# A two-layer encoder on one core: recurrent pairs back to back, neighbourhood values by four units, start stage in runs

## Chip, cores, metric

One NeuronCore of a Trainium2 chip runs the whole program in one launch. The metric is device time in microseconds (us), the median of several executions.

## What is computed

The input x is 1024 tokens by 1024 features, float32. Two residual layers follow each other, and a final RMS norm:

```python
h = rms_norm(x) * (1 + scale(c)) + shift(c)
x = x + gate(c) * mixer(h)          # shift, scale, gate: 1024x1024 products with silu(c)
# layer 0: differential attention (4 heads) beside a bidirectional RG-LRU (512 channels)
xc = conv4(xb);  a = exp(-8 * sigmoid(Wa xc) * softplus(-lam));  u = sqrt(1 - a*a) * sigmoid(Wx xc) * xc
y  = scan_forward(a0, u0) + scan_backward(a1, u1)
# layer 1: 16 heads of 2-D neighbourhood attention, 8 x 16 window, per-head bias
p  = softmax(q k^T * scale + bias + mask);  o = p v
# each group times silu of its own projection, then an output projection
```

The result has to keep float32 accuracy, so every product is made of three matmuls on operands split in a high and a low part (`mm3`, L196-199).

## The kernel before

Activations lie transposed, features on partitions, so a projection of 128 output features over 512 tokens is 8 steps of three matmuls 128x512 into one PSUM bank (24 matmuls, called a slab half here; a slab has two halves). Weights come as slabs 128x1024 (`raw`): ScalarE (ACT) rounds the high part (`whi`, L181), GpSimd (POOL) subtracts for the low part (`wlo`, L182). VectorE (DVE) and ACT take the results out of the banks. The order of each engine follows the order in which the code issues instructions, changed by `tc.high_priority` and `tc.issue_after`; a `Feed` of generators gives projections out in pieces between other work (`pump(ns)` gives pieces worth so many ns), and `weave` alternates the pieces of several generators.

The stages, with the times of the profiled execution:

- **Start, 0 to 79 us.** x is loaded; `squares` (L470) makes the sums of squares of each half of the tokens with squares on ACT or DVE in `SQ` = 4 buffers and matmuls against a column of ones into 32 rows each (`ss_add`, L321); `spread` (L350) copies the reciprocal roots to all partitions through the constant `sel`. `mod_first(g)` (L255), for g = 0 to 3, loads eight pieces of the modulation weights (`ada`) and multiplies each with c into 32 rows, piece by piece. `parts` makes the normalized, modulated and split activations (`ahi`, `alo`), `products` (L499) the products of the first three slabs: xb0, xb1 (recurrent input) and v0.
- **Recurrent branch, 79 to 242 us.** For each of four chunks of 128 channels: `conv` (L630) on DVE; `pair` (L661) takes two chunks: gate products into banks, sigmoid and tanh on ACT into tiles `t`, `w` of one ring of `LR` = 12 buffers (a pair holds 12), then exp, square, sqrt on ACT and multiplies and scans (L707 to L714) on DVE. `gb(c)` is the projection for the silu gate of a chunk, which multiplies the scanned result (L605, L722) and stores it to DRAM. `xb(c)` is the projection that gives a chunk's input, `vj(h)` that of a head's values, `kq0` that of the first head's keys and queries, `mods` sums of later modulations on DVE. The order is the list `jobs`:

```python
jobs = [weave(pair((0, 1)), chain(xb(2), xb(3))), cv(2), cv(3), vj(1), vj(2),
        gb(0), gb(1), weave(pair((2, 3)), chain(vj(3), kq0()), mods(...)), gb(2), gb(3)]
```

- **Differential attention** to 500 us and the first output layer to 640 us.
- **Neighbourhood attention, 640 to 1128 us.** 64 units (8 pairs of heads, two halves of the tokens, four blocks). `na_a(u)` makes the logits of two heads and the softmax on DVE, ACT and POOL; `na_b(u)` transposes the six 128-column tiles (`etr`, L1202) and copies them to `et`, one head on DVE (L1208), the other on ACT (L1206); `na_c(u)` multiplies them with the values into 64 columns of the array for each head (`no`, L1226), six matmuls a unit. The loop over u issues na_a(u+1), a pump of 1700 ns, na_b(u), a pump, na_c(u-1), a pump.
- **Second output layer** to the end.

Matmuls of `norm`, `mod` and `no` (and a few others) use a part of the array's columns, 32 or 64; those of projections, gates, logits and transposes use all 128. A run below is a row of such narrow matmuls with no other between them.

Of the kernel before, what the change touches and what calls it, by code (L numbers as in the profile page):

```python
# [27 lines left out]
SQ = 4  # L28
# [68 lines left out]
def kernel(ctx, tc, xT, xTp, small, lamp, adaw, tb, w0, gw, wo0, w1, nab, wo1, out):  # L97
# [28 lines left out]
    sel = const.tile([P, 4, P], F32, tag="sel", name="sel")  # L126
    G.memset(sel[:], 1.0)
    G.affine_select(sel[:], sel[:], pattern=[[-32, 4], [0, P]], base=0, channel_multiplier=1,
                    compare_op=ALU.is_equal, fill=0.0)
# [3 lines left out]
                    compare_op=ALU.is_equal, fill=0.0)  # L133

# [120 lines left out]
    def mod_first(g, pool, small, c32):  # L255

        ps = ptp.tile([P, HF], F32, tag="pt", name=f"mod{g}")

        def sums(x, w, start, stop):
            for n in range(4):  # L260
                cols = x[:, n // 2, (n % 2) * P:(n % 2 + 1) * P]
                state["modmm"] = T.matmul(ps[32 * n:32 * n + 32, :P], w, cols,
                                          start=start, stop=stop)

        for k in range(KC):
# [3 lines left out]
            sums(piece, c32[:, k, :], k == 0, k == KC - 1)  # L269
        row = pool.tile([P, P], F32, tag="mrow", name="mrow", bufs=2)  # L270
        A.activation(row[:], ps[:, :P], AF.Copy)
        pc = ps[:, P:]
        T.matmul(pc[:, :4], row[:], pick[:], start=True, stop=True)
        m = small.tile([P, 2, 2], F32, tag=f"first{g}", name=f"first{g}", bufs=1)
        gain = small.tile([P, 2], F32, tag=f"gain{g}", name=f"gain{g}", bufs=1)
        b = sm[:, O_ADAB:O_ADAB + 2 * KC].rearrange("p (t k) -> p t k", t=2)
        V.tensor_tensor(m[:], pc[:, :4].rearrange("p (t j) -> p t j", t=2),
                        b[:, :, 2 * g:2 * g + 2], ALU.add)
        V.scalar_tensor_tensor(gain[:], m[:, 1, :], 1.0, sm[:, O_NG + 2 * g:O_NG + 2 * g + 2],
                               ALU.add, ALU.mult)  # L280
        for j in range(2):
            first_mod[2 * g + j] = gain[:, j:j + 1], m[:, 0, j:j + 1]
# [38 lines left out]
    def ss_add(ss, sq, start, stop, w=P):  # L321
        for j in range(4):
            T.matmul(ss[32 * j:32 * j + 32, :w], ones[:], sq[:, j * w:(j + 1) * w],
                     start=start, stop=stop)
# [25 lines left out]
    def spread(rr, bc, w=P):  # L350
        for j in range(4):
            T.matmul(bc[:, j * w:(j + 1) * w], sel[:, j, :], rr[:, :w], start=True, stop=True)
# [105 lines left out]
    with tc.tile_pool(name="start", bufs=2) as stp, tc.tile_pool(name="ada0", bufs=12) as adp:  # L458
        mixp[1] = stp
        for k in range(KC):  # L460
            mix_tile(k, f"xT{k}")
# [8 lines left out]
        def squares(hf, on_dve, pool, tag):  # L470
            for k in range(KC):
                state["x"] = nc.sync.dma_start(half(k, hf), xT[k * P:(k + 1) * P,
                                                               hf * HF:(hf + 1) * HF])
            ss = nbank[hf] = pool.tile([P, HF], F32, tag=tag, name=f"norm{hf}")
            for k in range(KC):
# [5 lines left out]
                ss_add(ss, sq, k == 0, k == KC - 1)  # L481
# [17 lines left out]
        def products(i, g, hf):  # L499
# [7 lines left out]
            for k in (2 * g, 2 * g + 1):  # L507
                mm3(banks[i, hf], ready[i][0][:, k, :], ready[i][1][:, k, :],
                    hact[k, hf][0][:], hact[k, hf][1][:], k == 0, k == KC - 1)
# [17 lines left out]
        products(2, 0, 0)  # L527
        with tc.issue_after(state["x"].ins):
            mod_first(2, adp, stp, c32)
        for i in range(3):  # L530
            products(i, 0, 1)
        for g in range(1, KC // 2):
# [5 lines left out]
            for n in range(6):  # L538
                i, hf = divmod(n, 2) if g == KC // 2 - 1 else (n % 3, n // 3)
                products(i, g, hf)  # L540
        for i, evac in enumerate((evac_xb(0), evac_xb(1), evac_v(0))):
            for hf in range(2):
                evac(hf, banks[i, hf])
        ahead(3)
# [81 lines left out]
    with tc.tile_pool(name="lru", bufs=1) as lp:  # L626
# [3 lines left out]
        def conv(c):  # L630
# [4 lines left out]
            eng = V if c < 2 else G  # L635
            eng.tensor_scalar(xc[:], x[:], cw(2), sm[:, O_CB + c:O_CB + c + 1], ALU.mult, ALU.add)
# [7 lines left out]
            V.tensor_copy(xh[:], xc[:])  # L644
# [89 lines left out]
        def weave(*jobs):  # L734

            jobs = list(jobs)
            while jobs:
                for job in tuple(jobs):
# [3 lines left out]
                    else:  # L742
# [17 lines left out]
    with ExitStack() as l0:  # L760
        ap = l0.enter_context(tc.tile_pool(name="attn", bufs=1))
        vtok = {}

# [267 lines left out]
    with tc.tile_pool(name="bound", bufs=2) as bp:  # L1031
        run, tail = out_layer(0, ato0, xTp, x1d, bp, [4, 5, 6, 7, 0, 1, 2, 3], by_tile,
# [33 lines left out]
    with ExitStack() as l1:  # L1066
# [46 lines left out]
        def load_ahead(p, w8):  # L1113

            if f"1v{p + 1 - (p + 1) % 2}" in feed.done:
                for b in range(min(4, w8 - 1)):
                    load_v(p + 1, b)
# [32 lines left out]
        def load_bias(u):  # L1150
            if u == 8 * NA_PAIRS:
                return
# [3 lines left out]
            bias["next"] = ap.tile([P, 2, 384], F32, tag="bias", name="bias")  # L1156
            nc.sync.dma_start(bias["next"][:, :, :n],
                              nab[2 * p:2 * p + 2, hf, :, BLK_B[b]:BLK_B[b] + n].rearrange(
                                  "h p n -> p h n"))

        def na_a(u):
# [14 lines left out]
            e = ap.tile([P, 2, 384], F32, tag="e", name="e")  # L1176
# [4 lines left out]
            for m in range(2):  # L1181
                state["dve"] = V.tensor_tensor_reduce(  # L1182
                    out=e[:, m, :n], in0=ps[:, m, :n], in1=bias["now"][:, m, :n], scale=-1.0,
# [10 lines left out]
        def na_b(u, e):  # L1194
# [4 lines left out]
            et = ap.tile([P, 2, 384], F32, tag="et", name="et", bufs=2)  # L1199
# [4 lines left out]
            for m in range(2):  # L1204
                if m:
                    A.activation(et[:kn, m, :], pt[:kn, m, :384], AF.Copy)  # L1206
                else:
                    V.tensor_copy(et[:kn, m, :], pt[:kn, m, :384])  # L1208
            return et

        def na_c(u, et):
            p, w8 = divmod(u, 8)
            hf, b = divmod(w8, 4)
            kn = 4 * BLK_W[b]
            if w8 == 0:
                feed.upto(f"1v{p - p % 2}")
                for n in range(4):
                    load_v(p, n)
                if p == 0:
                    feed.pump(5000.0)  # L1220
            if b == 0:
                ob[0] = ptp.tile([P, HF], F32, tag="pt", name=f"no{u}")
            po = ob[0]
            for j in range(3):
                for m in range(2):
                    T.matmul(po[64 * m:64 * m + 64, b * P:(b + 1) * P],  # L1226
                             vch[p, b][:kn, j + hf, 64 * m:64 * m + 64],
                             et[:kn, m, j * P:(j + 1) * P], start=(j == 0), stop=(j == 2))
            if b == 3:
                if late(p):  # L1230
                    if hf == 0:
                        mix_tile(p, f"o1_{p}")
                    A.activation(mixed[p][:, hf * HF:(hf + 1) * HF], po[:], AF.Copy)
                    written.add((p, hf))
                    gate1(p, hf)
                else:
                    feed.upto(f"1g{p}")
                    m = mixed[p][:, hf * HF:(hf + 1) * HF]
                    V.scalar_tensor_tensor(m, po[:], 0.5, m, ALU.mult, ALU.mult)
            load_ahead(p, w8)  # L1240
# [4 lines left out]
        for u in range(n_units + 1):  # L1245
            if u + 1 < n_units:
# [4 lines left out]
            feed.pump(PUMP1 if u < 56 else 800.0)  # L1251
            if u:
                na_c(u - 1, ets.pop(u - 1))
            feed.pump(PUMP1 if u < 56 else 800.0)
# [5 lines left out]
    with tc.tile_pool(name="fin", bufs=2) as fp:  # L1260
# [6 lines left out]

        segments = ((0, 0, 0, 512), (0, 1, 0, 256), (0, 1, 256, 512))
# [109 lines left out]
```

## Time and profile before

| | |
|---|---|
| median of 3 runs | 1229.72 us (1228.05 to 1231.03) |
| profiled execution | 1229.11 us, its span 1227.2 us |
| mean granted TensorE clock | 0.995 |
| PE (matmul) busy | 96% of the span, 7232 instructions |
| DVE, ACT, POOL busy | 59%, 45%, 31% |

The profiled execution is 0.05% under the median and has 1.9 us around its span. PE's ends are modelled and successive matmuls overlap in the record, so PE's pace is read from start to start, and a stall from the idle time that stands in square brackets ahead of an instruction, with the instruction that released it.

### The profile page before, as it was taken

The page shows a single profiled execution, that of the slowest core. Times are in us where ns is not written, and L with a number is a line of the kernel's source. Part 1 is how long each engine was busy: PE and PEld are TensorE (multiplying, and loading weights), DVE is VectorE, ACT ScalarE, POOL GpSimd, SP SyncE. Part 2 cuts the span into 40 slices and gives each one's busy share as a digit, 9 for nine tenths or more (in the row PEclk, how much of TensorE's full clock was granted, in tenths as well). Part 3 has the DMA queues.
Part 4 walks back from the last instruction along what each step waited for, and adds up shares of the span by engine and source line. Part 5 has one row for each costly group of instructions (what it writes and reads, how often), then busy time and mean ns, then how long its engine had stood idle before and what let it go on. Part 6 is the DMA issues. An engine that isn't in the chain of part 4 may idle for free.

```text
span 1227.2 us, 19073 instructions
## 1 busy us (share of the span) xinstructions
PE 1177.9 (96%) x7232; PEld 969.2 (79%) x7232; DVE 725.6 (59%) x1418; ACT 553.5 (45%) x1023; POOL 376.3 (31%) x348
## 2 busy tenths in 40 slices
PE   4989999799999999999999999999999999999997
PEld 3578887678888888777778888888988898877896
DVE  6762966899899889668672433453333323464344
ACT  3337658456666556423342333443344324375121
POOL 2113432133243334533422323333323333244100
PEclk9999999999999999999999999999999999999999
DMA  9610153232123110286424443333332333223312
GB/s 330 188 38 27 60 170 105 69 101 78 42 63 108 46 57 20 84 284 205 149 72 149 124 145 109 117 116 108 100 108 81 103 105 106 76 81 113 136 69 70
DMA packets 81467, 132.24 MB, mean 108 GB/s; under 512 B 7008, under 2 KB 48096, under 8 KB 81376
## 3 DMA queue, kind: packets, MB, share of 16 engines
q1 hardware_dynamic: 81376, 131.03, 34.1%
q8 instruction: 57, 0.93, 0.3%
q14 instruction: 34, 0.28, 0.1%
HBM read 110.03 MB, written 14.68 MB: 102 GB/s over the span
## 4 chain that ended last, share of the span: by engine, by line
PE 82%; DVE 10%; DMA 3%; ACT 2%; POOL 1%; issue 1%; SPq 0%; DVEq 0%; ACTq 0%; POOLq 0%
PE pp L197 16%; PE pp L199 16%; PE pp L198 15%; PE no L1226 4%; PE etr L1202 3%; PE v L197 3%; PE v L198 2%; PE v L199 2%; PE atr L857 2%; PE s L599 2%; PE s L600 2%; PE n L599 2%; PE n L600 2%; PE o L198 1%; PE o L197 1%
## 5 line engine op out<-in xcount | busy, mean ns | idle before, releaser
L197 PE MATMUL pp<-ahi,whi 128*128 128x512 f32 (+1 forms) x1040 | 405.9, 390 | 3.7 <-DVE sgb L605 3.3
L199 PE MATMUL pp<-ahi,wlo 128*128 128x512 f32 (+1 forms) x1040 | 397.4, 382 | 2.5 <-POOL wlo L182 2.5
L198 PE MATMUL pp<-alo,whi 128*128 128x512 f32 (+1 forms) x1040 | 395.8, 381 | 0.0
L182 POOL TENSOR_TENSOR wlo<-raw,whi 128x1024 fp32r<-128x1024 f32 x80 | 196.1, 2454 | 333.5 <-ACT whi L181 330.0
L197 PEld LDWEIGHTS pp<-ahi,whi 128*128 128x128 f32 x1040 | 196.3, 189 | 45.8 <-issue 9.6
L199 PEld LDWEIGHTS pp<-ahi,wlo 128*128 128x128 f32 x1040 | 196.3, 189 | 41.1 <-POOL wlo L182 3.4
L198 PEld LDWEIGHTS pp<-alo,whi 128*128 128x128 f32 x1040 | 196.5, 189 | 32.2 <-issue 0.7
L1182 DVE CUSTOM_DVE_ANT_0 e<-n,bias 128x288 f32<-128x288 f32 (+1 forms) x128 | 60.4, 504 | 151.8 <-PE n L600 76.7
L181 ACT ACTIVATE whi<-raw 128x1024 fp32r<-128x1024 f32 x80 | 84.3, 1055 | 133.4 <-PE pp L198 88.2
L1190 POOL TENSOR_SCALAR e<-e,r 128x288 f32<-128x288 f32 (+1 forms) x128 | 72.3, 577 | 180.0 <-DVE r L1188 178.0
L1185 ACT ACTIVATE e<-e,nm 128x288 f32<-128x288 f32 (+1 forms) x128 | 72.8, 570 | 111.9 <-DVE nm L1182 111.2
L831 ACT ACTIVATE e<-e,nm 128x1024 f32<-128x1024 f32 x64 | 73.4, 1148 | 38.3 <-DVE nm L827 37.7
L827 DVE CUSTOM_DVE_ANT_0 e<-s,tb 128x1024 f32<-128x1024 f32 x64 | 76.9, 1216 | 3.9 <-DMA tb<-in_tb_dram 2.6
L197 PE MATMUL v<-whi,ahi 128*128 128x256 f32 x256 | 74.7, 292 | 0.0
L198 PE MATMUL v<-wlo,ahi 128*128 128x256 f32 x256 | 72.5, 283 | 0.0
L199 PE MATMUL v<-whi,alo 128*128 128x256 f32 x256 | 72.3, 282 | 0.0
L848 POOL TENSOR_SCALAR e<-e,r 128x256 f32<-128x256 f32 x32 | 32.9, 1028 | 100.6 <-DVE r L837 42.4
L1226 PE MATMUL no<-et,vc 96*64 96x128 f32 (+1 forms) x768 | 60.6, 282 | 0.0
L1226 PEld LDWEIGHTS no<-et,vc 96*64 96x64 f32 (+1 forms) x768 | 42.2, 136 | 21.5 <-issue 19.3
L864 ACT ACTIVATE ath<-atr 128x512 fp32r<-128x512 f32 x64 | 38.0, 596 | 45.7 <-PE atr L857 45.4
L1206 ACT ACTIVATE et<-etr 96x384 f32<-96x384 f32 (+1 forms) x64 | 31.2, 487 | 58.8 <-DVE et L1208 53.7
L962 DVE SCALAR_TENSOR_TENSOR xh<-pp,mod,xh 128x512 f32<-128x512 f32 (+1 forms) x40 | 25.7, 643 | 53.8 <-PE pp L199 47.7
(206 smaller groups left out, 2007.6 us busy)
## 6 DMA issues: line engine op xcount, KB each, us to landing
raw<-in_w_dram SPq DMA_DIRECT2D x56, 512.0 KB
ada<-in_adaw_dram SPq DMA_DIRECT2D x96, 256.0 KB
raw<-in_wo_dram SPq DMA_DIRECT2D x24, 512.0 KB
bias<-in_nab_dram SPq DMA_DIRECT2D x32, 288.0 KB
qq<-qq SPq DMA_DIRECT2D x48, 128.0 KB
bias<-in_nab_dram SPq DMA_DIRECT2D x16, 384.0 KB
xT<-in_xT_dram SPq DMA_DIRECT2D x16, 256.0 KB
xh<-in_xTp_dram SPq DMA_DIRECT2D x16, 256.0 KB
```

The lines of the kernel that those rows point to most:

```text
L181: A.activation(hi[:], raw[:], AF.Copy)
L182: G.tensor_tensor(lo[:], raw[:], hi[:], ALU.subtract)
L197: T.matmul(ps, lh, rh, start=start, stop=False)
L198: T.matmul(ps, lh, rl, start=False, stop=False)
L199: state["pe"] = T.matmul(ps, ll, rh, start=False, stop=stop).ins
L599: T.matmul(dst, qsel(q[m]), k, start=True, stop=False)
L827: state["dve"] = V.tensor_tensor_reduce(out=e[:], in0=ps[:].rearrange("p a b -> p (a b)"), in1=tbt[h][:, o:o + S], scale=-1.0, scalar=3.0e ...
L831: A.activation(e[:], e[:], AF.Exp, scale=-1.0, bias=nm[:], accum_out=sums[:, m:m + 1])
L1182: state["dve"] = V.tensor_tensor_reduce(out=e[:, m, :n], in0=ps[:, m, :n], in1=bias["now"][:, m, :n], scale=-1.0, scalar=3.0e38, op0=ALU.a ...
L1185: A.activation(e[:, m, :n], e[:, m, :n], AF.Exp, scale=-1.0, bias=nm[:, m:m + 1], accum_out=sums[:, m:m + 1])
L1190: state["pool"] = G.tensor_scalar(e[:, m, :n], e[:, m, :n], r[:, m:m + 1], 0.0, ALU.mult, ALU.add).ins
L1226: T.matmul(po[64 * m:64 * m + 64, b * P:(b + 1) * P], vch[p, b][:kn, j + hf, 64 * m:64 * m + 64], et[:kn, m, j * P:(j + 1) * P], start=(j ...
```

## The change

1. **Start.** `SQ` is 8. All eight pieces of a group g are loaded ahead (for odd g into buffers of another pool), and for g > 0 the sums of all pieces are issued in one run that begins with the piece that landed last; so are the sums of squares of the second half. `products` takes wh·hi, wl·hi, wh·lo in this order; slab v0 lags a step behind, and its last products come after xb0 and xb1 are taken out. `sel` is made anew in each of four stages.
2. **Recurrent branch.** The convolution's first operation and its rounding are on ACT for chunks 0 and 1. The jobs are in another order: pair (2,3) follows vj(1), with vj(2), gb(0), gb(1) woven in; gb(2), gb(3) come after vj(3) and the first keys and queries.
3. **Neighbourhood attention.** `na_c` multiplies four units in one run of 24 matmuls. The transposes' copies go back into `e` (5 buffers). The bias comes in a tile for each head. One pump of three times the size stands between na_a(u+1) and na_b(u).

```diff
-SQ = 4
+SQ = 8
...
         for k in range(KC):
-            piece = pool.tile([P, 2, 2 * P], F32, tag="ada", name="ada")
+            where, tag, bufs = pool, "ada", KC
+            if g % 2:
+                where, tag, bufs = kqp, ("qq0", "qq1", "qlo")[k // 3], 3
+            piece = where.tile([P, 2, 2 * P], F32, tag=tag, name="ada", bufs=bufs)
...
+            with tc.high_priority():
+                sums(pieces[KC - 1], c32[:, KC - 1, :], True, False)
+                with tc.issue_after(state["modmm"].ins):
+                    for k in range(KC - 1):
+                        sums(pieces[k], c32[:, k, :], False, k == KC - 2)
...
+            if hf:
+                ss_add(ss, sqs[KC - 1], True, False)
+                with tc.issue_after(state["ssmm"].ins):
+                    for k in range(KC - 1):
+                        ss_add(ss, sqs[k], False, k == KC - 2)
...
-            eng = V if c < 2 else G
-            eng.tensor_scalar(xc[:], x[:], cw(2), sm[:, O_CB + c:O_CB + c + 1], ALU.mult, ALU.add)
+            if c < 2:
+                A.activation(xc[:], x[:], AF.Identity, scale=cw(2),
+                             bias=sm[:, O_CB + c:O_CB + c + 1])
...
-        jobs = [weave(pair((0, 1)), chain(xb(2), xb(3))), cv(2), cv(3), vj(1), vj(2),
-                gb(0), gb(1),
-                weave(pair((2, 3)), chain(vj(3), kq0()),
-                      mods(NM[0], kqp, tag="qq0", bufs=3, acc=(lp, "macc"), wait=NW[0])),
-                gb(2), gb(3)]
+        jobs = [proj(at0[c_xb + 2], 0, evac_xb(2)),
+                weave(pair((0, 1)), chain(proj(at0[c_xb + 2], 1, evac_xb(2)), xb(3))),
+                cv(2), cv(3), vj(1),
+                weave(pair((2, 3)), chain(vj(2), gb(0), gb(1))),
+                weave(chain(vj(3), kq0()), mod), gb(2), gb(3)]
...
+            po = ptp.tile([P, HF], F32, tag="pt", name=f"no{u}")
+            for b in range(4):
+                kn = 4 * BLK_W[b]
+                for j in range(3):
+                    for m in range(2):
+                        T.matmul(po[64 * m:64 * m + 64, b * P:(b + 1) * P],
+                                 vch[p, b][:kn, j + hf, 64 * m:64 * m + 64],
+                                 ets[b][:kn, m, j * P:(j + 1) * P],
+                                 start=(j == 0), stop=(j == 2))
...
+            if u and u % 4 == 0:
+                na_c(u - 4, [ets.pop(u - 4 + b) for b in range(4)])
...
             if u + 1 < n_units:
                 es[u + 1] = na_a(u + 1)
-            feed.pump(PUMP1 if u < 56 else 800.0)
+            feed.pump(3 * pump)
             if u < n_units:
                 ets[u] = na_b(u, es.pop(u))
```

Three places in the order of the engines. PE in the start stage, before (`start` are products of the first slabs, `mod` the sums of the third group of modulation pieces):

```order
L199 MATMUL start_456<-ahi_0_637,wlo_388 128x512
L262 MATMUL mod_581<-ada,c_125 32x128 x4
L197 MATMUL start_456<-ahi_0_642,whi_387 128x512
L198 MATMUL start_456<-alo_0_643,whi_387 128x512
L262 MATMUL mod_581<-ada,c_125 32x128 x4
L199 MATMUL start_456<-ahi_0_642,wlo_388 128x512
L197 MATMUL start_499<-ahi_0_637,whi_463 128x512
L262 MATMUL mod_581<-ada,c_125 32x128 x4
```

and now:

```order
L537 MATMUL start_555<-alo_1_490,whi_294 128x512
L535 MATMUL start_555<-ahi_1_494,whi_294 128x512
L536 MATMUL start_555<-ahi_1_494,wlo_295 128x512
L537 MATMUL start_555<-alo_1_495,whi_294 128x512
L265 MATMUL mod_499<-ada,c_125 32x128 x32
L537 MATMUL start_456<-alo_1_490,whi_387 128x512
```

The four matmuls of each piece stood apart between products; the 32 of a group now stand together. Counted over the whole order, the narrow runs are 123 before (19 of `mod`, 5 of `norm`, 76 of `no`, 23 others) and 62 now (5, 2, 32 and the same 23).

ACT in the recurrent branch, before: the square roots of pair (0,1) (`w<-w`), then both halves of gb(0) and gb(1) (`sgb`), then the first sigmoids of pair (2,3) (L678):

```order
L704 ACTIVATE w<-w 128x1024 x3
L181 ACTIVATE whi_1301<-raw_1243 128x1024
L377 ACTIVATE vT_1237<-pp_1_1245 128x512
L604 ACT_TABLE_LOAD
L604 ACTIVATE sgb<-pp_0_1271 128x512
L181 ACTIVATE whi_1367<-raw_1305 128x1024
L604 ACTIVATE sgb<-pp_1_1307 128x512
L604 ACTIVATE sgb<-pp_0_1337 128x512
L181 ACTIVATE whi_1462<-raw_1371 128x1024
L604 ACTIVATE sgb<-pp_1_1373 128x512
L678 ACT_TABLE_LOAD
L678 ACTIVATE t_1403<-gate,sm 128x512 x2
```

and now (the sigmoids are L721):

```order
L747 ACTIVATE w<-w 128x1024 x3
L394 ACTIVATE vT_1259<-pp_0_1218 128x512
L747 ACTIVATE w<-w 128x1024
L721 ACT_TABLE_LOAD
L721 ACTIVATE t_1212<-gate,sm 128x512 x2
L721 ACTIVATE t_1236<-gate,sm 128x512 x2
```

The sigmoids of pair (2,3) follow the last square root of pair (0,1) at once. They write into the ring's buffers that pair (0,1) holds.

PE in the neighbourhood attention, before, around one unit's values:

```order
L198 MATMUL pp_0_6217<-alo_0_5522,whi_5991 128x512
L199 MATMUL pp_0_6217<-ahi_0_5521,wlo_5992 128x512
L1226 MATMUL no_6254<-et,vc_0_6197 64x128 x6
L197 MATMUL pp_1_6261<-ahi_1_5711,whi_5991 128x512
L198 MATMUL pp_1_6261<-alo_1_5712,whi_5991 128x512
```

and now:

```order
L202 MATMUL pp_0_6282<-ahi_0_5527,wlo_5992 128x512
L1250 MATMUL etr_6319<-ident,e 96x128 x6
L1268 MATMUL no_6331<-e,vc_0_6242 64x128 x6
L1268 MATMUL no_6331<-e,vc_1_6247 64x128 x6
L1268 MATMUL no_6331<-e,vc_2_6252 64x128 x6
L1268 MATMUL no_6331<-e,vc_3_6257 64x128 x6
L635 MATMUL n_6357<-ks_5637,qq_5833 128x384
```

The values of four units stand together, directly behind the transposes of the fourth, whose copies the last six of the run read; before, a pump stood between a unit's transposes and its values. The last seven units before the end of the stage have no projections left, and most of their narrow runs stay (18 of `no`).

## Rows read from the trace of the kernel before

**Rows 1.** The page: PE's busy time (the rest of that line is PE's weight loads and the other engines), and the shares of the chain of work that ended last.

```profile
PE 1177.9 (96%) x7232; PEld 969.2 (79%) x7232; DVE 725.6 (59%) x1418; ACT 553.5 (45%) x1023; POOL 376.3 (31%) x348
...
PE 82%; DVE 10%; DMA 3%; ACT 2%; POOL 1%; issue 1%; SPq 0%; DVEq 0%; ACTq 0%; POOLq 0%
```

**Rows 2.** The waits of PE over the whole span, the one of the gate products: engine, tile and line that waited, what for, us in total, times, longest.

```profile
PE gate L197 <- DVE xch L644: 3.8, 1, 3.8
```

**Rows 3.** Timeline of PE in the neighbourhood attention: start us, us, engine, line, operation, out<-in, count, and in brackets idle time before it and its releaser.

```profile
701.99 0.39 PE L199 MATMUL pp<-ahi,wlo 128*128 128x512 f32 x1
702.31 0.88 PE L1226 MATMUL no<-et,vc 96*64 96x128 f32 x12
703.12 0.50 PE L197 MATMUL pp<-ahi,whi 128*128 128x512 f32 x1
703.45 0.39 PE L198 MATMUL pp<-alo,whi 128*128 128x512 f32 x1
```

**Rows 4.** The tile `no`: its weight loads on PE (count, min/median/max ns), and the time in which they sat idle before them, in how many cases.

```profile
L1226 PEld LDWEIGHTS no<-et,vc x768: 132/137/137, 679.0 to 1127.6; 96*64 96x64 f32 x96, 128*64 128x64 f32 x96
...
  issue: 19.3, 62
```

**Rows 5.** Timeline of PE in the start stage, modulation sums between products.

```profile
51.04 0.86 PE L262 MATMUL mod<-ada,c 128*32 128x128 f32 x24
...
54.44 0.40 PE L199 MATMUL start<-ahi,wlo 128*128 128x512 f32 x1
54.77 0.43 PE L262 MATMUL mod<-ada,c 128*32 128x128 f32 x8
55.13 0.50 PE L197 MATMUL start<-ahi,whi 128*128 128x512 f32 x1
55.46 0.40 PE L198 MATMUL start<-alo,whi 128*128 128x512 f32 x1
```

**Rows 6.** Timeline of ACT in the start stage: squares of the second half, then the third slab's high part.

```profile
27.07 1.65 ACT L480 ACTIVATE sq<-xT 128x512 f32<-128x512 f32 x3
31.32 1.15 ACT L480 ACTIVATE sq<-xT 128x512 f32<-128x512 f32 x2 [2.60 <-PE norm L323]
32.38 1.04 ACT L181 ACTIVATE whi<-raw 128x1024 fp32r<-128x1024 f32 x1
```

**Rows 7.** Timeline of PE in the start stage: the first product with the third slab's low part, the spread of the second half's norm, and the first product that follows it.

```profile
35.92 0.50 PE L199 MATMUL start<-ahi,wlo 128*128 128x512 f32 x1 [0.30 <-POOL wlo L182]
...
38.95 1.16 PE L352 MATMUL norm<-rr,sel 128*128 128x128 f32 x8
...
42.22 0.50 PE L197 MATMUL start<-ahi,whi 128*128 128x512 f32 x1 [1.09 <-ACT ahi L360]
```

**Rows 8.** Timeline of DVE: the convolution of chunks 0 and 1.

```profile
75.24 2.51 DVE L636 TENSOR_SCALAR xc<-xb,sm 128x1024 f32<-128x1024 f32 x1 [9.39 <-ACT xb L370]
77.78 4.62 DVE L640 SCALAR_TENSOR_TENSOR xc<-xb,sm,xc 128x1022 f32<-128x1022 f32 x2
82.32 0.81 DVE L636 TENSOR_SCALAR xc<-xb,sm 128x1024 f32<-128x1024 f32 x1
83.04 2.47 DVE L640 SCALAR_TENSOR_TENSOR xc<-xb,sm,xc 128x1023 f32<-128x1023 f32 x2
```

**Rows 9.** Windows: us, busy time (and instructions) of PE, PE's loads, DVE, ACT, POOL, then PE's granted clock as a share of 2.4 GHz, DMA share, GB/s.

```profile
86.00:88.00 2.00, 1.83 (x4) 1.49 (x5) 2.00 (x4) 0.00 (x0) 0.00 (x0) 0.50 0.00 0
88.00:90.00 2.00, 2.00 (x8) 1.57 (x7) 1.90 (x3) 0.00 (x0) 0.00 (x0) 0.75 0.00 0
232.00:236.00 4.00, 1.90 (x8) 1.60 (x9) 4.00 (x3) 0.92 (x1) 2.64 (x1) 1.00 0.00 0
240.00:242.00 2.00, 1.14 (x5) 0.96 (x6) 1.38 (x2) 0.08 (x1) 0.00 (x0) 1.00 0.66 258
652.00:656.00 4.00, 3.89 (x20) 3.63 (x18) 0.92 (x3) 1.01 (x4) 1.44 (x3) 0.57 0.72 233
```

**Rows 10.** Timeline of PE at the end of the recurrent branch.

```profile
234.10 0.50 PE L197 MATMUL pp<-ahi,whi 128*128 128x512 f32 x1 [3.33 <-DVE sgb L605]
...
240.86 0.50 PE L599 MATMUL s<-ks,qq 128*128 128x512 f32 x1 [2.84 <-DVE sgb L605]
```

**Rows 11.** Timeline of ACT and DVE for pair (0,1): the last sigmoid, the first scan, and the last sum of a forward and a backward scan.

```profile
121.86 0.69 ACT L678 ACTIVATE t<-gate,sm 128x512 f32<-128x512 f32 x1
...
139.00 2.29 DVE L710 TENSOR_TENSOR_SCAN t<-t,t 128x1024 f32<-128x1024 f32 x1
...
156.81 1.22 DVE L714 TENSOR_TENSOR t<-t,w 128x1024 f32<-128x1024 f32 x1
```

**Rows 12.** Timeline of PE: the first transposes of the neighbourhood attention, and the product before them.

```profile
649.18 0.28 PE L197 MATMUL v<-whi,ahi 128*128 128x256 f32 x1
651.71 1.52 PE L1202 MATMUL etr<-ident,e 128*96 128x128 f32 x6 [2.25 <-POOL e L1190]
```

**Rows 13.** Timeline of PE, DVE and ACT around one unit's transposes and their two copies.

```profile
706.71 0.82 PE L1202 MATMUL etr<-ident,e 128*128 128x128 f32 x6
...
707.28 0.47 PE L197 MATMUL pp<-ahi,whi 128*128 128x512 f32 x1
...
707.56 0.56 DVE L1208 COPY et<-etr 128x384 f32<-128x384 f32 x1 [0.71 <-PE etr L1202]
...
708.21 0.49 ACT L1206 ACTIVATE et<-etr 128x384 f32<-128x384 f32 x1 [0.50 <-DVE r L1188]
```

More of the change, by code (lines that the diff above doesn't have):

```diff
@@ L133, with make_sel @@
                     compare_op=ALU.is_equal, fill=0.0)
+    def make_sel(pool):
+        sel = state["sel"] = pool.tile([P, 4, P], F32, tag="sel", name="sel", bufs=1)
+        G.memset(sel[:], 1.0)
+        G.affine_select(sel[:], sel[:], pattern=[[-32, 4], [0, P]], base=0,
+                        channel_multiplier=1, compare_op=ALU.is_equal, fill=0.0)
     mixed = {}
@@ L351, in spread @@
         for j in range(4):
-            T.matmul(bc[:, j * w:(j + 1) * w], sel[:, j, :], rr[:, :w], start=True, stop=True)
+            T.matmul(bc[:, j * w:(j + 1) * w], state["sel"][:, j, :], rr[:, :w], start=True, stop=True)
     def make_h(l, k, hf, x, bc):
@@ L456, in small_constants @@
         V.tensor_scalar(nl[:], nl[:], -0.2, None, ALU.add)
-    with tc.tile_pool(name="start", bufs=2) as stp, tc.tile_pool(name="ada0", bufs=12) as adp:
+    with tc.tile_pool(name="start", bufs=2) as stp, tc.tile_pool(name="ada0", bufs=KC) as adp:
         mixp[1] = stp
+        make_sel(stp)
         for k in range(KC):
@@ L526 @@
         parts(0, 1)
-        products(2, 0, 0)
         with tc.issue_after(state["x"].ins):
             mod_first(2, adp, stp, c32)
-        for i in range(3):
+        for i in range(2):
             products(i, 0, 1)
+        rest = [(2, 0, 0), (2, 0, 1)]
         for g in range(1, KC // 2):
@@ L537 @@
                 parts(g, hf)
[L538 to L541, printed above, removed]
+            for i in range(2):
+                for hf in range(2):
+                    products(i, g, hf)
+            for args in rest:
+                products(*args)
+            rest = [(2, g, 0), (2, g, 1)]
+        for i, evac in enumerate((evac_xb(0), evac_xb(1))):
             for hf in range(2):
                 evac(hf, banks[i, hf])
+        for args in rest:
+            products(*args)
+        for hf in range(2):
+            evac_v(0)(hf, banks[2, hf])
         ahead(3)
@@ L1155, in load_bias @@
             n = 12 * BLK_W[b]
[L1156 to L1159, printed above, removed]
+            bias["next"] = []
+            for m in range(2):
+                t = ap.tile([P, 384], F32, tag="bias", name="bias", bufs=3)
+                nc.sync.dma_start(t[:, :n], nab[2 * p + m, hf, :, BLK_B[b]:BLK_B[b] + n])
+                bias["next"].append(t)
         def na_a(u):
@@ L1175, in na_a @@
             nm = ap.tile([P, 2], F32, tag="nm", name="nm")
-            e = ap.tile([P, 2, 384], F32, tag="e", name="e")
+            e = ap.tile([P, 2, 384], F32, tag="e", name="e", bufs=5)
             for m in range(2):
@@ L1205, in na_b, with na_c @@
                 if m:
-                    A.activation(et[:kn, m, :], pt[:kn, m, :384], AF.Copy)
+                    A.activation(e[:kn, m, :], pt[:kn, m, :384], AF.Copy)
                 else:
-                    V.tensor_copy(et[:kn, m, :], pt[:kn, m, :384])
-            return et
-        def na_c(u, et):
+                    V.tensor_copy(e[:kn, m, :], pt[:kn, m, :384])
+            return e
+        def na_c(u, ets):
             p, w8 = divmod(u, 8)
[L1213 to L1240, printed above, removed]
@@ L1242 @@
+            if late(p):
+                if hf == 0:
+                    mix_tile(p, f"o1_{p}")
+                A.activation(mixed[p][:, hf * HF:(hf + 1) * HF], po[:], AF.Copy)
+                written.add((p, hf))
+                gate1(p, hf)
+            else:
+                feed.upto(f"1g{p}")
+                m = mixed[p][:, hf * HF:(hf + 1) * HF]
+                V.scalar_tensor_tensor(m, po[:], 0.5, m, ALU.mult, ALU.mult)
         n_units = 8 * NA_PAIRS
@@ L1245 @@
         for u in range(n_units + 1):
+            pump = PUMP1 if u < 56 else 800.0
+            if u and u % 4 == 0:
+                na_c(u - 4, [ets.pop(u - 4 + b) for b in range(4)])
+            if u % 8 == 3:
+                p = u // 8
+                feed.upto(f"1v{p - p % 2}")
+                for b in range(4):
+                    load_v(p, b)
+            elif u >= 8:
+                load_ahead(u // 8 - 1)
             if u + 1 < n_units:
                 es[u + 1] = na_a(u + 1)
-            feed.pump(PUMP1 if u < 56 else 800.0)
+            feed.pump(3 * pump)
             if u < n_units:
                 ets[u] = na_b(u, es.pop(u))
[L1251 to L1254, printed above, removed]
             after_dve(mod, 1)
```

47 lines of the change are left out of this document (32 added, 15 removed).

## Prediction

> **What bounds the kernel.** The page comes first [rows 1]: PE is busy for 96% of the span, and the chain that ended last is 82% PE, 10% DVE. The change leaves PE's matmuls as they are, so it can save only time in which PE stands, issues slower than it could, or runs at half clock. The busy share doesn't show how much that is: a product is recorded as 0.39 us but its successor starts 0.23 us later [rows 3], so busy time overlaps and covers small gaps. I therefore read the timeline from start to start.
>
> The first thing to see there is the price of a narrow run. From the last product ahead of the values of a unit (701.99) to the second product behind them (703.45) pass 1.46 us [rows 3]. Two product steps are 0.46. The twelve value records cost about 0.055 each (0.88 less the 0.27 of the last one, over 11), 0.66. So 0.34 us go into switching to narrow columns and back, seen as the steps of 0.32 and 0.33 beside them. The weight loads tell the same: idle before 62 runs for 19.3 us, 0.31 each [rows 4]. In the start stage, two products with eight modulation records between them take 55.46 less 54.44, 1.02 us [rows 5]; 0.46 is the products', 0.21 the records' (24 of them took 0.43 longer than 8), 0.35 the switch. I take 0.35 a run, 0.31 as the lower end.
>
> The second is PE's longer stalls: 3.76 us at the first gates [rows 2, 8], 3.33 and 2.84 at the end of the recurrent branch [rows 10], 2.25 at the first transposes [rows 12]. The third is the clock behind them [rows 9]: after the first and the last of these the granted clock was at 0.50 and 0.57, the lower of its levels for most of the window (1.2 of 2.4 GHz); after the other two it stayed at 1.00.
>
> **The change, part by part.** The sum is made against the profiled execution, 1229.1 us, which is 0.6 under the median shown.
>
> *Start: -5.7 (from -3 to -8).* ACT stands for 2.60 us before its last squares because four buffers wait for sums on PE [rows 6]. Behind that come, one after the other, the third slab's high part, its low part, for which PE waits, and the root and spread at 38.95, for which PE stands another 1.09 [rows 7]. With eight buffers the 2.60 goes; I take 2.5 off all that follows. From 42 to 57 us the pieces of the last two groups of modulations come in 11 runs; in two runs they cost 9 x 0.35 = 3.2 less. Against it stands a new wait: a run starts only when its last piece is in, and the products queued behind on PE wait with it. The loads have buffers of their own now, so I put it at nothing; if a load comes late it is at most what the first part gives (the -3). The other narrow runs that go lie where PE waits for ACT and DVE anyway: nothing. Making `sel` again is POOL work (31% busy), needed tens of us later: nothing. The order of the two high products changes no count.
>
> *First gates: -5.3 (from -1.5 to -5.6).* PE stood 3.76 us, and the windows at 0.50 and 0.75 lost 2 x 0.50 + 2 x 0.25 = 1.5 more. Both go if the chain from xb0 to the rounded convolution is covered. PE now has 66 products between xb0's first half and the first gate (18 of its other half and xb1, 24 of v0, 24 of the next slab), 66 x 0.227 = 15.0 us. The chain: two evictions of 0.60 and a slab's rounding of 1.04 between, ACT's first operation (about 1.1, from the 1.04 of another 1024-wide one), three of 1.24 on DVE, ACT's rounding of 1.1, together 8.1; if DVE is held as at 75.24, where an operation took 2.51 that elsewhere took 0.81, and two took 4.62 instead of 2.47 [rows 8], 3.9 more, 12.0. Covered either way; if the cover failed by the whole stall, 1.5 of the gain would be left.
>
> *End of the branch: -6.2.* The two stalls come from gb(2), gb(3) queued on DVE behind the scans. From the last sigmoid of pair (0,1) to its last scan sum passed 36 us [rows 11]. Behind the last gates of pair (2,3) PE now has a third of the woven 144 products (48; each of 16 gate products takes six with it) and the 144 of vj(3), keys and queries, 192 x 0.227 = 43.6 us. Both stalls go.
>
> *New wait at the gates of pair (2,3): +3.7 (from 0 to +9.3).* The ring holds 12 tiles, all taken by pair (0,1), so the first new sigmoid waits for its first scan, and PE for the banks that ACT doesn't empty. In the trace that scan ended at 141.3, 18.7 us after the last sigmoid [rows 11]. Between lie the 48 products of vj(1), 10.9 us, and what PE does ahead until four banks are full, four rounds of three gate and six other products, 4 x 9 x 0.227 = 8.2. I take half of it, 4.1, because the evictions of those other products queue on ACT behind the waiting sigmoid. That leaves 3.7; with the whole cover nothing, without any 7.8. After stalls of 3.33 and 2.84 the clock stayed up [rows 9]. The Trainium skill (TensorE: Matmul & The Clock Gate, section on HAM oscillation) tells of waits of a few us between matmuls that each bring the engine back to half clock; by that rule 1.5 us more would be lost and the sum would be 1200.7; the trace shows it after two stalls of four. I keep the 1.5 for the upper end, 9.3.
>
> *Values by four units: -15.4 (at 0.31: -13.6).* 76 runs become 32; 44 x 0.35.
>
> *First transposes: -4.0.* PE stood 2.25 us for POOL, and four us at 0.57 lost 1.7 [rows 9, 12]. A pump of 3 x 1700 ns lies between now, so the stall and its half clock go.
>
> *Copies in front of the values: +3.0 (from 0 to +16).* Before, a pump lay between a unit's transposes and its values. Now the last six matmuls of a run need both copies, which ended 1.99 us after the first transpose (706.71 to 708.70) [rows 13]. PE reaches them 0.57 + 0.2 + 18 x 0.11 = 2.75 us after it. So nothing, unless evictions of a projection stand ahead of the copies: keys or queries put about 1.3 us there (two of ACT, two of DVE), a wait of 0.6, in perhaps 5 of the 16 runs. At 1 us in each it would be 16.
>
> *Smaller edits.* Bias by head makes more transfers of half the size on a queue with time left; the copies and their work are the same. At the end of the stage the run of the last four units still waits for the last copies as before. Nothing each.
>
> Sum: -5.7 - 5.3 - 6.2 + 3.7 - 15.4 - 4.0 + 3.0 = -29.9, 1229.1 - 29.9 = **1199.2 us**.
>
> **Rivals.**
> (A) *The copies are late in every run.* For it: copies run one after the other on two engines that also empty the projections' banks. Against it: ACT and DVE are busy 45 and 59% [rows 1]. 16 instead of 3: 1212.
> (B) *Pair (2,3) waits for all of pair (0,1), not its first scan.* Up to 156.8 instead of 141.3 [rows 11]: 15.5 to 20 us more at the gates, and the last scans then come late again for gb(2), gb(3), whose 6.2 isn't gained: about 1222. For it: a ring hands buffers out in order, and its third tile is the forward result, kept until its store. Against it: gates stand woven with products, so PE goes on until banks run out.
> (C) *The price isn't one of a run.* Narrow matmuls themselves may be slow, and merging them saves nothing: without 15.4 and 3.2, 1218. Against it: 0.31 to 0.35 for twelve records of 64 columns and for eight of 32, beside them and not in them. The Trainium skill says the same (TensorEngine Tiling (Array Packing), Key Properties): changing the tiling mode drains TensorE, going to another tile doesn't. By that rule C is out; the trace agrees with 0.32 before and 0.33 after a run.
> (D) *Slower: values' waits that also drop the clock.* If copies queue behind keys' evictions and a slab's rounding (1.04), and the wait reaches the 2.25 us behind which the clock fell [rows 12], each of 16 runs costs 2.25 + 1.5, 60 instead of 3: 1256. It decides from (29.9 + 3.0) / 16 = 2.06 us a run. Against it: a stall of 1.09 [rows 7] is the nearest in size to what the queues suggest.
> (E) *No change that can be told.* A measurement here resolves about 0.2%, 2.5 us. It needs several bad ends together: A and B.
>
> **How the numbers follow.** The forecast 0.65, A 0.13, B 0.08, C 0.05, D 0.05, E 0.04. Faster by over 0.2%: the forecast, A, B, C, 0.91; same 0.04; slower 0.05. The forecast's own bounds: from start -8, no new wait, no wait for copies, 1190, to start -3, first gates -1.5, the new wait 9.3 and 0.31 a run, 1213. The range reaches from 1188, for gains in stages that I left at nothing, to 1219, which takes in A and C; B, D and E are left out.
>
> **What would show it.** Right: `mod` in four to five runs and start products that end near 72 instead of 79; no PE wait for the rounded convolution; PE waits of 3 to 4 us at the sigmoids of pair (2,3); none for `sgb`; `no` in groups of 48 records; no wait at the first transposes, and waits of PE on the copies (lines of `e`) of 3 us in all. Wrong: PE's wait on copies over 10 us, a stall over 10 us at pair (2,3), or steps of 0.6 or more beside a run of values.

## The result and the profile after

The changed kernel takes 1233.23 us (median of 7, 1230.77 to 1235.7), the kernel before 1228.05 (7 runs). The ratio is 1.0033, interval 1.0019 to 1.0047: slower by about 0.3%, where 2.4% faster was forecast. The profiled execution took 1230.93 us, its span 1229.2, the mean granted clock 0.979 against 0.995.

The page's lines that answer to [rows 1]: PE is busy 12.5 us less, yet the span is 2 us longer, and PE's share of the chain fell from 82% to 71%.

```profile
PE 1165.4 (95%) x7232; PEld 982.2 (80%) x7232; DVE 724.1 (59%) x1414; ACT 546.7 (44%) x1020; POOL 383.8 (31%) x354
...
PE 71%; DVE 8%; DMA 5%; issue 3%; ACT 3%; POOL 2%; SPq 0%; DVEq 0%; POOLq 0%; ACTq 0%
```

PE's waits over the span (what waited, for what: us in total, times, longest), those that matter here. The gates' wait for `xch` of [rows 2] is gone, and so are the waits for `sgb` of [rows 10]. All of these are new, and the first two matter most:

```profile
PE mrow L340 <- DVE macc L314: 13.9, 3, 10.1
...
PE no L1268 <- DMA vc<-vd: 5.3, 2, 4.6
...
PE gate L200 <- ACT vT L394: 2.9, 1, 2.9
...
PE etr L1250 <- ACT e L1254: 2.0, 1, 2.0
PE n L635 <- DVE nm L1231: 1.8, 2, 1.3
...
PE gate L200 <- ACT t L721: 1.3, 1, 1.3
```

`macc` is the sum of a part of the later modulations, made on DVE from eight pieces (`mod_part`); `mrow` is PE's matmul that follows it. PE around the longest wait: the attention's first value transposes, then the matmul, then a product.

```profile
214.35 1.03 PE L817 MATMUL vtr<-ident,vT 128*128 128x128 f32 x8
225.44 0.66 PE L340 MATMUL mrow<-macc,ones 128*32 128x128 f32 x8 [10.05 <-DVE macc L314]
226.02 0.80 PE L200 MATMUL pp<-ahi,whi 128*128 128x512 f32 x1
```

DVE ahead of the first wait, at 188.99 (3.00 us), waits for a piece of weights itself; ahead of the long one the additions of the sum (L314) stand between the multiplies and scans of pair (2,3) (L750 to L757), and the last two come at 223.75.

```profile
185.24 3.60 DVE L314 SCALAR_TENSOR_TENSOR macc<-ada,ctmp,macc 128x512 f32<-128x512 f32 x2 [0.58 <-DMA ada<-in_adaw_dram]
...
204.31 2.29 DVE L753 TENSOR_TENSOR_SCAN t<-t,t 128x1024 f32<-128x1024 f32 x1
206.51 2.33 DVE L750 TENSOR_TENSOR t<-t,w 128x1024 f32<-128x1024 f32 x2
208.77 2.28 DVE L755 TENSOR_TENSOR_SCAN w<-t,t 128x1024 f32<-128x1024 f32 x1
210.97 4.42 DVE L753 TENSOR_TENSOR_SCAN t<-t,t 128x1024 f32<-128x1024 f32 x1
...
217.56 0.74 DVE L314 SCALAR_TENSOR_TENSOR macc<-ada,ctmp,macc 128x512 f32<-128x512 f32 x1
218.22 2.28 DVE L755 TENSOR_TENSOR_SCAN w<-t,t 128x1024 f32<-128x1024 f32 x1
220.42 0.72 DVE L314 SCALAR_TENSOR_TENSOR macc<-ada,ctmp,macc 128x512 f32<-128x512 f32 x1
...
223.75 1.53 DVE L314 SCALAR_TENSOR_TENSOR macc<-ada,ctmp,macc 128x512 f32<-128x512 f32 x2
```

The first run of values, behind the transposes of the fourth unit: the two waits inside it are for the values' load.

```profile
687.51 0.82 PE L1250 MATMUL etr<-ident,e 128*96 128x128 f32 x6
688.25 1.31 PE L1268 MATMUL no<-e,vc 96*64 96x128 f32 x20
690.22 0.88 PE L1268 MATMUL no<-e,vc 128*64 128x128 f32 x12 [0.65 <-DMA vc<-vd]
695.71 2.09 PE L1268 MATMUL no<-e,vc 128*64 128x128 f32 x16 [4.61 <-DMA vc<-vd]
697.73 0.69 PE L635 MATMUL n<-ks,qq 128*128 128x384 f32 x1
```

Behind each of these waits PE ran at half clock (granted 0.50, that is 1.2 of 2.4 GHz). Windows as in [rows 9], the clock third from the end; they follow the waits of 2.90 at the gates, 3.00 and 10.05 at `mrow`, and 4.61 at the values:

```profile
128.00:132.00 4.00, 2.70 (x6) 1.70 (x7) 4.00 (x2) 3.92 (x5) 0.00 (x0) 0.50 0.00 0
...
189.00:191.00 2.00, 2.00 (x11) 1.35 (x12) 1.93 (x4) 1.52 (x3) 0.00 (x0) 0.50 0.93 255
...
225.00:229.00 4.00, 3.56 (x15) 2.64 (x16) 2.35 (x4) 2.81 (x5) 0.00 (x0) 0.50 0.30 66
...
696.00:700.00 4.00, 4.00 (x22) 3.27 (x20) 1.28 (x4) 0.00 (x0) 0.00 (x0) 0.50 0.63 208
```

### The profile page after: what moved, and what is told of

It is laid out like the page before. It is cut to its first block, busy times and chain, and to the rows that moved or that the text cites. A ratio compares the mean times of both kernels' runs of the same rounds, so it can differ in the third digit from the quotient of the medians.

```text
span 1229.2 us, 19265 instructions
## 1 busy us (share of the span) xinstructions
PE 1165.4 (95%) x7232; PEld 982.2 (80%) x7232; DVE 724.1 (59%) x1414; ACT 546.7 (44%) x1020; POOL 383.8 (31%) x354
## 4 chain that ended last, share of the span: by engine, by line
PE 71%; DVE 8%; DMA 5%; issue 3%; ACT 3%; POOL 2%; SPq 0%; DVEq 0%; POOLq 0%; ACTq 0%
PE pp L200 14%; PE pp L201 14%; PE pp L202 14%; PE no L1268 4%; PE etr L1250 3%; PE v L200 2%; PE v L202 2%; PE v L201 2%; DMA ada<-in_adaw_dram 2%; PE atr L903 2%; PE s L635 2%; PE s L636 2%; PE n L635 2%; PE n L636 1%; PE o L201 1%
## 5 line engine op out<-in xcount | busy, mean ns | idle before, releaser
L200 PE MATMUL pp<-ahi,whi 128*128 128x512 f32 (+1 forms) x1040 | 400.9, 386 | 0.0
L1256 DVE COPY e<-etr 96x384 f32<-96x384 f32 (+1 forms) x64 | 35.5, 554 | 134.7 <-PE etr L1250 128.1
L1254 ACT ACTIVATE e<-etr 96x384 f32<-96x384 f32 (+1 forms) x64 | 31.2, 487 | 88.7 <-DVE e L1256 84.6
L1268 PE MATMUL no<-e,vc 96*64 96x128 f32 (+1 forms) x768 | 52.3, 280 | 5.3 <-DMA vc<-vd 5.3
L314 DVE SCALAR_TENSOR_TENSOR macc<-ada,ctmp,macc 128x512 f32<-128x512 f32 x56 | 47.4, 847 | 14.6 <-DMA ada<-in_adaw_dram 14.2
L1250 PE MATMUL etr<-ident,e 128*96 128x128 f32 (+1 forms) x384 | 53.2, 273 | 2.9 <-ACT e L1254 2.0
```

What stands on the lines that cost most here:

```text
L200: T.matmul(ps, lh, rh, start=start, stop=False)
L1250: T.transpose(pt[:kn, m, j * P:(j + 1) * P], e[:, m, j * kn:(j + 1) * kn], ident[:])
L1268: T.matmul(po[64 * m:64 * m + 64, b * P:(b + 1) * P], vch[p, b][:kn, j + hf, 64 * m:64 * m + 64], ets[b][:kn, m, j * P:(j + 1) * P], start ...
```

## The experiments

The theory after this reading: the parts that were priced gave about what was forecast, and new waits of PE that were not priced ate it, above all the one for `macc`. The rivals stand in the expectations. Each ratio is to the kernel before on the same chip (medians there 1229.1, 1228.6 and 1230.0).

**One part alone, three times.** The edits are the parts 1, 2 and 3 of the change as listed above, each put into the kernel before; the third takes `sel` per stage with it.

> The kernel before with the change's first part alone (squares in eight buffers, modulation sums in runs, slab v0 a step behind, sel per stage). Theory 1 (each part keeps in the whole what it does alone, and new waits of PE in the other parts ate the gain): the start's products end 5.6 us earlier, as in the changed kernel, and the convolution starts earlier by more than that since xb0 and xb1 are taken out ahead of v0's last products, so 1228.0 becomes 1219 to 1222.5. Theory 2 (what is won at the start is lost at the next wait): within 2 us of 1228.

Measured: 1225.39 us, ratio 0.997 (0.9953 to 0.9986), 3.7 us faster. This lies between the two theories: theory 1 asked for 5.5 to 9, theory 2 for 2 at most. In its trace the start's last product begins at 73.60, 5.25 us ahead of the kernel before, and the first transposes of the attention come 4.7 us earlier. By the first logits of the neighbourhood attention 0.2 of it is left (642.68 against 642.91); in the first output layer between them PE waited 3.9 us for another `macc`, which it does not do there in the kernel before.

> The kernel before with the second part alone (convolution's first operation and rounding on ACT, the new order of jobs). Theory 1: the recurrent branch is where the time is lost. PE waits some 13 us for the modulation sums (macc) that DVE has queued among the scans of pair (2,3), some 6 us at the gates of pair (2,3), and loses several us at half clock behind them; the old stalls of 3.5 and 3.0 go. 1238 to 1246. Theory 2 (the loss lies elsewhere, as in the neighbourhood attention): 1220 to 1229.

Measured: 1243.66 us, ratio 1.0118 (1.0096 to 1.0139), 14.5 us slower, as theory 1 said. The loss is in this part. Of its waits:

```profile
PE mrow L323 <- DVE macc L297: 13.3, 2, 10.6
...
PE gate L197 <- ACT vT L377: 2.9, 1, 2.9
```

> The kernel before with the third part alone (values by four units, copies back into e, bias by head, one pump; and sel per stage, which makes the room). Theory 1: 44 runs fewer save about 14 us, the wait for the first values' load and its half clock take 6 to 8 of it, stalls in the last 30 us of the stage 4: net -4 to -8, 1220 to 1224. Theory 2 (a run of narrow matmuls costs nothing, the switch is paid by each matmul): the waits alone, +6 to +12, 1234 to 1240.

Measured: 1223.87 us, ratio 0.9968 (0.9957 to 0.9979), 5.3 us faster: theory 1. The three parts add to -3.7 + 14.5 - 5.3 = +5.5; the whole change measured +5.2.

**The modulation sums back beside pair (2,3).**

```diff
-                weave(pair((2, 3)), chain(vj(2), gb(0), gb(1))),
-                weave(chain(vj(3), kq0()), mod), gb(2), gb(3)]
+                weave(pair((2, 3)), chain(vj(2), gb(0), gb(1)), mod),
+                chain(vj(3), kq0()), gb(2), gb(3)]
```

> The changed kernel with the modulation sums woven with pair (2,3) as before, instead of with vj(3) and the keys and queries. Theory 1: PE's waits for macc (3.0 and 10.1 us) go with some 4 us of half clock behind them, 1233.2 becomes 1216 to 1221. Rival (DVE's scans are the bound of this stage, the sums only sit on the same queue): the scans end as late as ever, PE waits for sgb or for the attention's first logits instead, 1228 to 1233.

Measured: 1220.45 us, ratio 0.9931 (0.9914 to 0.9948), 12.8 under the changed kernel. The wait of 10 us is gone and did not come back at `sgb` or the first logits; one of 3.2 stays. The last sum of a forward and a backward scan even ended later than in the changed kernel (228.37 against 223.84), and PE did not wait for it. So the scans were not the bound; the modulation sums only stood in the wrong place among them. This one move turns the change from slower to faster.

```profile
PE no L1268 <- DMA vc<-vd: 5.0, 1, 5.0
...
PE mrow L340 <- DVE macc L314: 3.2, 1, 3.2
```

**A pump ahead of the first values** (on top of e4; the runs after it are on top of e5):

```diff
+            if u == 4:
+                feed.pump(5000.0)
             if u and u % 4 == 0:
                 na_c(u - 4, [ets.pop(u - 4 + b) for b in range(4)])
```

> The kernel with the early modulation sums (e4) and a pump of 5000 ns ahead of the first run of values, as the kernel before had one there. Theory 1: the wait of 5 us for the first values' load (vc) and the half clock behind it go, 1220.5 becomes 1213.5 to 1215.5. Rival (the projections given out there are missing as cover later, at the end of the stage where none are left): the stalls of the last 30 us grow by as much, 1219 to 1221.

Measured: 1213.92 us, ratio 0.9872 (0.9848 to 0.9896), 6.5 under e4: the wait of 5.0 and its half clock. The last 30 us did not pay for it.

**The price of a run, measured by itself.**

```diff
             for b in range(4):
+                if b:
+                    feed.pump(PUMP1 if u < 56 else 800.0)
                 kn = 4 * BLK_W[b]
...
-            feed.pump(3 * pump)
+            feed.pump(2.25 * pump)
```

> As e5, but a pump stands between the four units inside each run of values, taken from the pumps of the units (2.25 in place of 3), so that the runs of value matmuls are 71 instead of 32 in the order, with nothing else changed. Theory 1 (0.35 us a run for switching to narrow columns and back): 39 x 0.35 = 13.7 us slower than e5, 1226 to 1230. Rival C of the prediction (the price is not one of a run): within 3 us of e5.

Measured: 1224.15 us, ratio 0.9971 (0.995 to 0.9992), 10.2 above e5. 39 runs more (71 instead of 32 in the trace too) cost 0.26 us each, from a difference of two medians with some 3 us of scatter; by the two ratios to the kernel before it is 12.2 us, 0.31 each. In the traces the weight loads of `no` sat idle 15.9 us before 55 runs, against 5.5 before 26 in e5. That is a little less than the 0.31 to 0.35 read from the timeline, or the same, and rival C is out. The same switch in the changed kernel's start stage, one run of 64 modulation records between products:

```profile
49.12 0.39 PE L536 MATMUL start<-ahi,wlo 128*128 128x512 f32 x1
49.44 1.96 PE L265 MATMUL mod<-ada,c 128*32 128x128 f32 x64
51.32 0.50 PE L537 MATMUL start<-alo,whi 128*128 128x512 f32 x1
51.66 0.40 PE L535 MATMUL start<-ahi,whi 128*128 128x512 f32 x1
```

From 49.12 to 51.66 pass 2.54 us; two products (0.46) and 64 records at 0.027 (1.73) leave 0.35, as much as around 8 records [rows 5]. The price is one of a run, here the same for 8 records and for 64.

**vj(2) ahead of pair (2,3).**

```diff
-                cv(2), cv(3), vj(1),
-                weave(pair((2, 3)), chain(vj(2), gb(0), gb(1)), mod),
-                chain(vj(3), kq0()), gb(2), gb(3)]
+                cv(2), cv(3), vj(1), vj(2),
+                weave(pair((2, 3)), chain(gb(0), gb(1), vj(3)), mod),
+                kq0(), gb(2), gb(3)]
```

> As e5, and vj(2) goes back ahead of pair (2,3), with gb(0), gb(1), vj(3) woven in. Theory 1: 10.9 us more of products lie between the last sigmoid of pair (0,1) and the first gates of pair (2,3), more than the 5.2 us that PE waits there (3.06 and 2.16), so these waits and the half clock behind them (3 us) go: 6 to 9 us less than e5. Rival (the scans of pair (2,3) end later by as much, gb(2) and gb(3) wait for them as before): not more than 3 us less than e5.

Measured: 1214.58 us, ratio 0.9884 (0.9857 to 0.9911), no better than e5. PE's waits at the gates went, but one of 7.41 us took their place. PE:

```profile
145.90 0.79 PE L200 MATMUL pp<-ahi,whi 128*128 128x512 f32 x1 [7.41 <-DVE sgb L641]
```

and DVE, where the silu of gb(0) (L641) stands behind the scans of pair (0,1):

```profile
136.01 2.26 DVE L753 TENSOR_TENSOR_SCAN t<-t,t 128x1024 f32<-128x1024 f32 x1
...
140.56 2.29 DVE L755 TENSOR_TENSOR_SCAN w<-t,t 128x1024 f32<-128x1024 f32 x1
...
145.16 0.68 DVE L641 SCALAR_TENSOR_TENSOR sgb<-sgb,pp 128x512 f32<-128x512 f32 x1
```

Neither theory had named this: it is the scans of pair (0,1), not of (2,3), that gb(0) now meets.

**Half of vj(2) ahead of pair (2,3).**

```diff
-                cv(2), cv(3), vj(1),
-                weave(pair((2, 3)), chain(vj(2), gb(0), gb(1)), mod),
+                cv(2), cv(3), vj(1), proj(at0[c_v + 2], 0, evac_v(2)),
+                weave(pair((2, 3)), chain(proj(at0[c_v + 2], 1, evac_v(2)), gb(0), gb(1)), mod),
```

> As e5, but the first half of vj(2) (24 products, 5.4 us) goes ahead of pair (2,3), the second half stays woven in with gb(0), gb(1). Theory 1: 5.4 us is just more than PE's 3.05 and 2.14 at the gates, so these go with the 3 us of half clock behind them, while gb(0) comes 5.4 us of products later than in e6, where PE waited 7.4 us for its eviction (sgb): 5 to 8 us less than e5's 1213.9, 1206 to 1209. Rival (gb(0)'s eviction waits for the scans of pair (0,1) whenever the gates don't): PE waits for sgb instead, 1212 to 1215.

Measured: 1208.53 us, ratio 0.9819 (0.9798 to 0.984), 5.4 under e5, in the range of theory 1, and the fastest version: 21 us under the kernel before. One wait of 1.8 for a sigmoid is left at the gates, and no wait for `sgb`. The 5.4 are not the gates' alone: in its trace the wait for `macc`, 3.3 in e5 with the clock at 0.50 behind it, is 2.3 with the clock at 1.00 behind it.

**The sum's matmul later.**

```diff
-NW = (3, 3, 3, 3)
+NW = (8, 3, 3, 3)
```

> As e5, with eight steps instead of three between the last modulation sum on DVE and its matmul on PE (NW[0]): the second mrow stands 29 rows, some 6 us of products, later on PE. Theory 1: the wait for macc of 3.3 us goes, with some 2 us of half clock: 1208 to 1211. Rival (the sum is late by more than 6 us, or the wait moves to what is queued behind): 1212 to 1215.

Measured: 1221.17 us, ratio 0.9927 (0.9903 to 0.9951), 7.3 above e5, against both expectations. PE's waits for `macc` came to 3.5, and new ones for evictions on DVE came (3.2 for keys, 2.2 for `sgb`). The sums share one buffer, which is free for the next only after the matmul; that a later first matmul (163.1 instead of 151.0) thereby pushes the second sum into the scans is argued from the code and not shown.

**Both together.** The edits of the last two runs, on top of e5.

> As e5, with the changes of e10 and e11 together. Theory 1: the gains add, 1200 to 1205. Rival: one of the two waits comes back in the other's place, 1207 to 1212.

Measured: 1211.72 us, ratio 0.9851 (0.982 to 0.9882), in the rival's range. It is 3.2 above e10, but the two intervals overlap: that the gains don't add is shown, that the later matmul costs here too is not. PE waited 5.2 us for `macc`, 4.4 of it at once.

## Why the prediction was wrong, point by point

- **Start, -5.7: right.** The last product begins at 73.23 instead of 78.85, 5.6 earlier. The spread of the second half's norm comes at 36.54 instead of 38.95 [rows 7], 2.4 earlier, and the matmul behind the last modulation run at 52.35 instead of 58.20; that is the waiting ACT and the fewer runs, as said. The part alone made the whole 3.7 faster (e1).
- **First gates, -5.3: right.** They start at 78.90 without a wait. e1, which lacks the convolution on ACT, still waits 3.8 there for the rounded convolution, and e2, which has it, does not (1.2 for the low part).
- **End of the branch, -6.2: the step that failed.** The waits for `sgb` went as said. But the step counted only what covers the scans on PE, and nothing of what moved beside them: `mods`, woven with pair (2,3) before and with vj(3) and the first keys and queries now, puts sixteen steps of sums on DVE in front of and among the multiplies and scans of pair (2,3), and PE's two matmuls behind them. The new place is in the diff, and no term priced it. PE stood 3.0 and 10.05 us for it and ran at half clock after each. e2 shows the loss in this part (+14.5), e4 that moving the sums back returns 12.8. In the kernel before PE came to the same two matmuls without a wait:

```profile
186.31 0.43 PE L323 MATMUL mrow<-macc,ones 128*32 128x128 f32 x8
...
209.05 0.43 PE L323 MATMUL mrow<-macc,ones 128*32 128x128 f32 x8
```

- **Wait at the gates of pair (2,3), +3.7 (to 9.3): near in size, by luck; the mechanism was another.** PE stood 2.90 and 1.30 us, 4.2 together; a third wait, 1.09 for a gate weight, was not foreseen. The prediction has the first new sigmoid wait for the first scan of pair (0,1), whose buffer in the ring it takes. In the trace ACT never stands for it:

```profile
127.90 0.80 PE L200 MATMUL gate<-xch,gwh 128*128 128x512 f32 x1 [2.90 <-ACT vT L394]
...
130.85 0.79 PE L200 MATMUL gate<-xch,gwh 128*128 128x512 f32 x1 [1.30 <-ACT t L721]
```

```profile
124.42 2.95 ACT L747 ACTIVATE w<-w 128x1024 f32<-128x1024 f32 x3
127.27 0.58 ACT L394 ACTIVATE vT<-pp 128x512 f32<-128x512 f32 x1
127.75 1.04 ACT L747 ACTIVATE w<-w 128x1024 f32<-128x1024 f32 x1
128.81 1.28 ACT L721 ACT_TABLE_LOAD   x1
130.11 1.84 ACT L721 ACTIVATE t<-gate,sm 128x512 f32<-128x512 f32 x3
```

The 2.90 ended when ACT took values of vj(1) out of a bank (`vT`), which stood behind three square roots of pair (0,1). The 1.30 ended with the first sigmoid, which follows the last square root and a table load without a pause. The first scan ended at 130.07 on DVE, just before that sigmoid, so it would have held the sigmoid to nearly the same time, but it did not make the longer wait. The clock was at 0.50 from 128 to 132. Its 1.5 had been kept for the upper end only, since it had stayed up after two of four stalls in the trace of before. By the rule of the Trainium skill that the prediction cites (TensorE: Matmul & The Clock Gate, HAM oscillation) it falls behind such waits. Here the trace agrees, with 0.50 in the windows behind 2.90, 3.00, 4.61 and 10.05; the other runs agree in part (last section).

- **Values by four units, -15.4: right, -14.0 by the trace.** The tile `no` after, what its loads and matmuls sat idle for (us, times); the first line answers to the 19.3 of 62 in [rows 4]. From outside, e9 puts a run at 0.26 to 0.31 us, 11.4 to 13.6 for 44.

```profile
  issue: 5.3, 26
...
  DVE e L1256: 0.3, 1
...
  ACT e L1254: 0.2, 1
```

- **First transposes, -4.0: nearly all of it.** They come at 660.02 with a wait of 0.36 for POOL instead of 2.25, and the clock behind it is at 1.00 (655 to 665): 1.9 and the 1.7 of half clock, 3.6.
- **Copies, +3.0: too much.** The other two lines are all that waited for them, 0.5 at most; the cover held, and by these waits the evictions ahead of the copies were hardly in the way.
- **Smaller edits, nothing: two things that no term names.** The old `na_c` had a pump of 5000 ns between issuing the loads of the first pair's values and using them. The change drops it. It also needs the values of four units within one run, at 688 to 697, where the kernel before came to them at 679.0, 686.7, 694.4 and 702.3. PE waited 5.3 us for these loads, and e5, which puts a pump back, returns 6.5; no run tells the missing pump from the earlier need. Near the end of the stage, waits of 2.0 (transposes for a copy on ACT) and 1.3 (logits for DVE, which waited for a bias) are new, and no run here tells what they are worth.
- **Rivals.** A did not happen (0.5 us), B did not (the longest gate wait is 2.9), C is excluded by e9, D's mechanism of waits and half clock is the right one at another place: not at the copies, but at `macc` and at the values' load. E came nearest in size (0.3% slower), but it was to need A and B together, and neither came. Of the signs of being wrong, "a stall over 10 us at pair (2,3)" came only in a way: 10.05 us, for sums that stood among its scans, not at its gates.

The terms, with what the two profiled executions show: -5.6, -5.3, -6.2, -14.0 for the runs, and -3.6 for the transposes, together about -35; against them 13.1 at `mrow`, 5.3 at the gates and 5.3 at the values, about 4 near the end of the stage, and 2 to 3 us of half clock behind each of four waits, together about 38. That leaves 3; the profiled executions differ by 1.8, the medians by 5.2. The list is rough: behind waits of 2.8 at the attention's first logits and 2.0 in an output layer the clock was at 0.56 and 0.57 too (259.7 to 263.5, 526 to 530), some 1.7 us each that the profiled execution of before does not have.

By stages it is plainer where the time went. PE's first gates come 7.3 us earlier than before (78.90 against 86.17), the first transposes of the attention's weights 10.3 later (269.73 against 259.40), the last values of the neighbourhood attention 4.1 later, and the end 2.0 later. The loss is in the recurrent branch, and the gain of the neighbourhood attention does not make up for it.

## What to carry to other kernels

When a job list is reordered, write down for every generator on it which engines' queues it enters and who waits for its last instruction; a small sum on an engine full of scans can hold the matmul engine longer than the scans themselves do. Merging narrow matmuls into longer runs was worth about 0.3 us a run here, if the work that stood between them doesn't also cover a load. Look for removed lines that seem to only pace the work: a pump that is taken out may have been somebody's cover.

## What the runs showed of the hardware

The switch between full and narrow columns cost 0.34 to 0.35 us around 8 [rows 5] and around 64 records of 32 columns, and around 12 of 64 columns [rows 3].

After a stall of PE the granted clock fell or stayed, and at some 3 us its length does not tell which. Behind 3.3 us for `sgb` it was at 1.00 in the kernel before [rows 9, 10] and in e3 (233 to 236), and at 0.50 in e1 (230 to 233). Behind 3.2 to 3.3 us at `mrow` it was at 1.00 in e9 (177.6 to 181) and at 0.50 in e5 (175 to 180), and the code of these two is the same up to there. Behind the longer ones past the start stage, 4.61 and 10.05 in the changed kernel, 4.96 in e4 (681 to 686), 5.32 in e3 (687 to 691) and 7.41 in e6 (146 to 149), it was at 0.50 each time. So a stall of some 3 us has to be priced with and without its half clock, and a longer one with it; here that was 2 to 3 us more.
